# One pass over the weights for both token segments of the residual products

## The chip, the cores and the metric

The kernel runs on one core of a Trainium2 chip. The metric is the time of one execution in device microseconds. On the core, TensorE (PE) multiplies matrices, with a weight load (PEld) beside each multiplication; VectorE (DVE), ScalarE (ACT) and GpSimd (POOL) work elementwise; the queue of SyncE (SP) issues the transfers. Each engine takes its instructions in the order in which the program lists them and waits on semaphores for the others.

## The reference, cut to what matters

Two layers work on 512 latent tokens and 256 context tokens with 1024 features. Each layer has a token mixing and a gated network with a short convolution, and each of the two ends in a residual product. These two products and the norm that follows each are what the change touches:

```
yl = concat([oa_l, ob_l, oc_l, od_l]) @ w_out[l]        # 1024 x 1024
xl = xl + g1 * yl
fl = modulate(rmsnorm(xl, norm_ffn_w[l]), sh2, sc2)
xl = xl + g2 * conv_ffn(fl, ...)                        # ends with @ ffn_w_down[l], 2816 x 1024
if need_ctx:                                            # not in the last layer
    xc = xc + cg1 * (concat([oa_c, ...]) @ w_out[l])    # the same for the context tokens
    ...
return rmsnorm(xl, final_norm_w)
```

The norm divides each token by the root of the mean of its squares over the 1024 features, so none of a token's features can be normed before all eight blocks of 128 features are there.

## The kernel before

Features lie on the partitions, in eight blocks of 128 (m or k = 0 to 7), and tokens along the free dimension. In layer 0 the tokens are two segments, 0 to 512 (latent) and 512 to 768 (context); in layer 1 only the 512 latent tokens are left, in two halves of 256. The residual stream is `x[m]`, 128x768 in float32.

Every product is made in three multiplications per block of 128 features: high part of the weights by high part of the input, high by low, and low by high. A weight unit (128 output features) is loaded by SP as `raw` (three buffers, loaded ahead in the order of `unit_order`), ACT casts it to the high part `wh` (L480), and POOL, or DVE and POOL together in the "fast" form, subtract to get the low part `wl` (L485). `wh` and `wl` have two buffers each; a "spare" unit takes the two buffers of the pool `mrow` instead, which the modulation rows (`mod_dve`, `junk`, L310) of layer 0 use too.

`w_out` (the product after the mixing, name `po`, 24 multiplications per unit and segment) and the last of the chunks of the down product in `ffn` (`pd`, 21 multiplications) run over all eight units for the first segment and then over all eight again for the second. So each unit is loaded, cast and split twice. After each product `residual` (L893, DVE) adds it to `x[m]`.

The norm is a generator, `norm_steps`: the squares `sq` (ACT) and their sums, which PE makes by multiplying with ones (`ms`); then `rstd` (ACT root, DVE reciprocal); then `rb`, the row spread to all partitions (PE); then eight steps of `norm_apply`, each with `yt` (DVE), the high part `yh` (ACT), and the low part `yl`, on DVE for even blocks and on POOL for odd ones (with a second `yt` there). `sq`, `yt` and the rows `up` and `ot` share the pool `u`, which has six buffers. `tick` takes steps of the first segment's norm between the products of the second sweep. With `direct` set, PE sums each square by itself; without it POOL or DVE add them first.

After the second segment's sweep its own norm begins, and `woven` puts the first products of the next stage between its steps: the up product (`pu`) after `w_out`, and the first input products of layer 1 (`pj`) after the down product of layer 0. The order of all this is the order in which the code issues it, apart from small moves by the scheduler.

Of the kernel before, what the change touches and what calls it, by code (L numbers as in the profile page):

```python
# [16 lines left out]
KT = 8  # L17
SEQ = 512
CTX = 256
T = SEQ + CTX  # L20
DEPTH = 2
DFF = 2816
NF = DFF // 128
# [12 lines left out]
SEGS = [(0, SEQ), (SEQ, T)]  # L36
HALVES = [(0, SEQ // 2), (SEQ // 2, SEQ)]
# [5 lines left out]
KEPT = (5, 7)  # L43
HEAD_START = 13
AHEAD_SCORES = 2
SCORE_SHARE = 0.4


# [4 lines left out]
class Trunk:  # L53
# [34 lines left out]
    def build(self):  # L88
# [40 lines left out]
        x = []  # L129
# [5 lines left out]
        steps = [self.rstd_steps(x, *sg, True, "tp", t) for sg, t in zip(SEGS, ("pv", "pj"))]  # L135
# [4 lines left out]
        y = self.new_y()  # L140
# [29 lines left out]
        for l in range(DEPTH):  # L170
            need = l < DEPTH - 1
            NT = T if need else SEQ
            fes.close()
            with ExitStack() as es:
                self.mixing_pools(es)
                todo = []
                if l == 0:
                    todo = list(range(8, 20))
                if l:
                    self.neg_lambda(l)  # L180
                self.mixing(l, y, need, todo)
# [11 lines left out]
            y = None  # L193
            for sg in segs:
                self.w_out(l, s, x, sg)
                y = y or self.new_y()
                steps = self.norm_steps(x, y, sg, self.affn[l], self.mod[l][:, 24:32], sg != segs[0])
                if sg == segs[0]:
                    self.pace = steps
                    self.tick(1)  # L200
            first = [self.up_open(l, 0, gv, True) for gv in range(2)]
            a, b = segs[0]
            part = lambda u, k0, k1: lambda: self.product(u[1][:, a:b], u[0], y, a, b, range(k0, k1))
            self.woven(steps, part(first[0], 0, 4), part(first[0], 4, 8), part(first[1], 0, 8))
            a, b = segs[1]
            self.pin = ALL
            for u in first:
                part(u, 0, 8)()
            self.pin = None
            todo = []  # L210
            if need:
                todo = [lambda j=j: self.mod_dve(0, j, 2) for j in range(40, 48)]
                todo += [lambda j=j: self.mod_dve(1, j, 2 if j < 16 else 1) for j in range(48)]
                self.cbc = self.cp.tile([128, 2, D], F32, name="cbc")
                self.load(self.cbc, d["cbc"], True)
                nc.scalar.activation(out=self.cbc, in_=self.cbc, func=AF.Silu)
            y2 = []

            def after(sg, l=l, need=need, x=x, y2=y2):
                if need:  # L220
                    if not y2:
                        self.scale_vec(l + 1, self.amix[l + 1], O_NM, 8)
                        y2.extend(self.new_y())
                    steps = self.norm_steps(x, y2, sg, self.amix[l + 1], self.mod[l + 1][:, 0:8], sg != segs[0])
                    if sg == segs[0]:
                        self.pace = steps
                        self.tick(1)
                    else:
                        early = self.early_start(l + 1, True)
                        part = lambda n, k0, k1: lambda: self.early_products([early[n]], y2, SEGS[0], range(k0, k1))  # L230
                        self.woven(steps, part(0, 0, 4), part(0, 4, 8), part(1, 0, 8))
                        self.early_products(early[1:], y2, SEGS[1], range(KT))
                        self.split_weights(spare=True)
                    if sg[1] <= SEQ:
                        for k in range(KT):
                            nc.sync.dma_start(out=xd[:, k, sg[0]:sg[1]], in_=x[k][:, sg[0]:sg[1]])
                else:
                    self.pace = self.final(x, sg, sg != segs[0])
                    self.tick(1 if sg == segs[0] else 99)

            self.ffn(l, x, y, segs, first, todo, after)
            y = y2
# [189 lines left out]
    def unit_order(self):  # L432

        for l in range(DEPTH):
            for u in UNITS:
                yield ("win", l, u)
            segs = SEGS if l < DEPTH - 1 else HALVES
            for _ in segs:
                for m in range(KT):
                    yield ("wout", l, m)  # L440
            for k0, k1 in CHUNKS:
                for i in range(k0, k1):
                    if i == 0:
                        yield ("wup", l, 0, 0)
                    yield ("wup", l, i, 1)
                    if i + 1 < NF:
                        yield ("wup", l, i + 1, 0)
                for _ in range(len(segs) if k1 == NF else 1):
                    for m in range(KT):
                        yield ("wdn", l, m, k0, k1)  # L450

    def prefetch(self, depth):
        while len(self.ahead) < depth:
# [284 lines left out]
    def mixing(self, l, y, need, todo):  # L738
# [66 lines left out]
        def score(n):  # L805
            nonlocal at
            for _ in range(n):
                if at < len(scores):
# [4 lines left out]
                    f()  # L813
                    after(w * SCORE_SHARE)

# [81 lines left out]
    def w_out(self, l, s, x, sg):  # L897
        a, b = sg
        for m in range(KT):
            w = self.weights(("wout", l, m), b - a == 256, m % 3 == 2 and l == 0)  # L900
            p = self.bank("tp", "po")
            self.product(p[:, :b - a], w, s, a, b)
            self.residual(p, x, self.mod[l][:, 16:24], m, a, b)
            self.tick(2 if m < 3 else 1)
        self.tick(KT)


    def up_open(self, l, i, gv, fast=False):
# [20 lines left out]
    def ffn(self, l, x, y, segs, first, todo, after):  # L929
        nc = self.nc  # L930
        NT = segs[-1][1]
        cseg = SEGS if NT == T else SEGS[:1]
        gate = self.mod[l][:, 40:48]
        def gate_unit(i):
            ug = self.up(l, i, 0, y, cseg, NT, None if i else first[0])
            nc.scalar.activation(out=ug[:, :NT], in_=ug[:, :NT], func=AF.Silu)
            return ug

        ug = gate_unit(0)
        for k0, k1 in CHUNKS:  # L940
            G = []
            for i in range(k0, k1):
                uv = self.up(l, i, 1, y, cseg, NT, None if i else first[1])
                eng = nc.vector if i == NF - 1 else nc.gpsimd
                cols = [(0, NT)] if eng is nc.vector else [(a, a + 256) for a in range(0, NT, 256)]
                for a, b in cols:
                    eng.tensor_tensor(out=uv[:, a:b], in0=ug[:, a:b], in1=uv[:, a:b], op=ALU.mult)  # L947
                gt = self.g.tile([128, 2, T], F32R, tag="g", name="g")
                nc.scalar.copy(out=gt[:, 0, :NT], in_=uv[:, :NT])
                for a, b in cols:  # L950
                    eng.tensor_tensor(out=gt[:, 1, a:b], in0=uv[:, a:b], in1=f32v(gt[:, 0, a:b]), op=ALU.subtract)  # L951
                G.append((gt[:, 0], gt[:, 1]))
# [5 lines left out]
            sweeps = [[sg] for sg in segs] if k1 == NF else [cseg]  # L958
            for sweep in sweeps:
                for m in range(KT):  # L960
                    w = self.weights(("wdn", l, m, k0, k1), sweep[0][1] - sweep[0][0] == 256,
                                     k1 == NF and m % 3 == 2 and l == 1)
                    for a, b in sweep:
                        p = self.bank("tp", "pd")
                        self.product(p[:, :b - a], w, G, a, b)
                        self.residual(p, x, gate, m, a, b)
                    if todo and m % 2:
                        todo.pop(0)()
                    self.tick(2 if m < 3 else 1)
                self.tick(KT)  # L970
                if k1 == NF:
                    after(sweep[0])


class Group:
# [436 lines left out]
```

## Time and profile before

| | us |
|---|---|
| median of 3 runs | 1759.32 (1756.22 to 1762.36) |
| the profiled execution | 1762.87 |
| its span in the trace | 1761.0 |
| PE busy | 1679.1 (95%) |
| DVE, ACT, POOL busy | 928.5, 787.5, 1017.3 |
| mean granted clock of PE | 0.986 |

The span is what the trace covers; 1.9 us of the execution lie around it. A row of a timeline gives the start, the duration, the engine, the line, what is written from what, and in brackets how long the engine sat idle before it and who released it.

### The profile page before, as it was taken

How to read it: one execution, taken by the hardware profiler on the slowest of the kernel's cores; microseconds unless marked ns; L12 is line 12 of the kernel's file. 1: busy time of each engine (PE TensorE's matmuls, PEld its weight loads, DVE VectorE, ACT ScalarE, POOL GpSimd, SP SyncE). 2: the span in 40 equal slices, each digit the busy share in tenths (PEclk: the TensorE clock that was granted, in tenths of full speed). 3: DMA queues.
4: the chain of work that ended last, by engine and by line, in shares of the span. 5: the costliest groups of instructions: out<-in, count | busy, mean ns of one | idle time of the engine just before them, and what ended most of it. 6: DMA issues, size and time to landing. Idle time of an engine off the chain costs nothing. (4 is left out here: it accounts for less than half of the span.)

```text
span 1761.0 us, 27484 instructions
## 1 busy us (share of the span) xinstructions
PE 1679.1 (95%) x10212; PEld 1448.2 (82%) x10212; DVE 928.5 (53%) x1789; ACT 787.5 (45%) x1355; POOL 1017.3 (58%) x1348
## 2 busy tenths in 40 slices
PE   7899999899999999999999988999999999999997
PEld 4578878798888888888888877888889888888887
DVE  3577767562767644543344566877656522122244
ACT  4377656553533311332133345776654543242343
POOL 1424235766678745775466664424865676676762
PEclk9999999999999999999999999999999999999998
DMA  8675545346533333343334536453436333333334
GB/s 334 177 217 188 156 115 179 93 122 231 168 108 121 124 113 98 120 131 110 119 111 135 181 113 188 138 150 102 147 109 221 106 99 90 102 93 99 96 114 127
DMA packets 78453, 244.21 MB, mean 139 GB/s; under 512 B 9072, under 2 KB 12656, under 8 KB 78192
## 3 DMA queue, kind: packets, MB, share of 16 engines
q1 hardware_dynamic: 78320, 242.46, 43.8%
q8 instruction: 81, 1.33, 0.3%
q14 instruction: 52, 0.43, 0.1%
HBM read 214.64 MB, written 27.79 MB: 138 GB/s over the span
## 5 line engine op out<-in xcount | busy, mean ns | idle before, releaser
L485 POOL TENSOR_TENSOR wl<-raw,wh 128x256 fp32r<-128x256 f32 (+1 forms) x750 | 575.2, 797 | 542.7 <-ACT wh L480 526.5
L480 ACT CAST wh<-raw 128x1024 fp32r<-128x1024 f32 (+1 forms) x228 | 233.5, 1027 | 422.7 <-PE pd L73 194.9
L73 PE MATMUL pu<-yh,wh 128*128 128x512 f32 (+1 forms) x1072 | 377.4, 352 | 1.8 <-DVE up L925 1.8
L73 PE MATMUL pu<-yl,wh 128*128 128x512 f32 (+1 forms) x1072 | 377.2, 352 | 1.8 <-POOL yl L411 1.5
L73 PE MATMUL pu<-yh,wl 128*128 128x512 f32 (+1 forms) x1072 | 376.3, 351 | 0.0
L73 PE MATMUL pd<-g,wh 128*128 128x512 f32 (+1 forms) x1168 | 290.9, 341 | 5.4 <-DVE x L893 2.4
L922 DVE SCALAR_TENSOR_TENSOR up<-pu,par,up 128x511 f32<-128x511 f32 (+1 forms) x132 | 83.0, 657 | 329.0 <-ACT up L920 329.0
L73 PEld LDWEIGHTS pd<-g,wh 128*128 128x128 f32 x1168 | 203.2, 192 | 31.1 <-ACT wh L480 5.6
L73 PEld LDWEIGHTS pu<-yh,wh 128*128 128x128 f32 x1072 | 202.7, 189 | 29.7 <-ACT wh L480 1.5
L73 PEld LDWEIGHTS pu<-yl,wh 128*128 128x128 f32 x1072 | 202.8, 189 | 29.3 <-POOL yl L411 2.1
L73 PEld LDWEIGHTS pu<-yh,wl 128*128 128x128 f32 x1072 | 202.7, 189 | 27.4
L73 PE MATMUL pj<-yh,wh 128*128 128x512 f32 (+1 forms) x608 | 217.4, 361 | 7.2 <-ACT ev L559 4.9
L73 PE MATMUL pj<-yl,wh 128*128 128x512 f32 (+1 forms) x608 | 213.6, 352 | 1.5 <-DVE yl L413 1.4
L73 PE MATMUL pj<-yh,wl 128*128 128x512 f32 (+1 forms) x608 | 212.4, 350 | 0.0
L73 PE MATMUL pd<-g,wl 128*128 128x512 f32 (+1 forms) x584 | 198.4, 341 | 4.6 <-DVE wl L485 4.5
L893 DVE SCALAR_TENSOR_TENSOR x<-pd,mod,x 128x512 f32<-128x512 f32 (+1 forms) x80 | 48.9, 614 | 181.9 <-PE pd L73 181.9
L73 PEld LDWEIGHTS pj<-yh,wh 128*128 128x128 f32 x608 | 117.1, 193 | 26.0 <-ACT ev L559 8.4
L73 PEld LDWEIGHTS pj<-yh,wl 128*128 128x128 f32 x608 | 117.2, 193 | 14.6
L655 POOL TENSOR_TENSOR p<-p,rec 128x512 f32<-128x512 f32 (+2 forms) x80 | 79.5, 997 | 85.6 <-DVE rec L651 62.6
L73 PEld LDWEIGHTS pj<-yl,wh 128*128 128x128 f32 x608 | 117.6, 193 | 13.2 <-DVE yl L413 3.1
L73 PEld LDWEIGHTS pd<-g,wl 128*128 128x128 f32 x584 | 112.3, 192 | 18.0 <-DVE wl L485 5.5
L310 DVE SCALAR_TENSOR_TENSOR junk<-mrow,cbc 128x1024 f32<-128x1024 f32 x80 | 123.2, 1541 | 1.4 <-DMA mrow<-in_wmodt 0.5
(176 smaller groups left out, 2750.5 us busy)
## 6 DMA issues: line engine op xcount, KB each, us to landing
raw<-in_wup SPq DMA_DIRECT2D x88, 512.0 KB, 3.5
mrow<-in_wmodt SPq DMA_DIRECT2D x56, 512.0 KB, 3.8
raw<-in_win SPq DMA_DIRECT2D x44, 512.0 KB, 3.7
raw<-in_wdn SPq DMA_DIRECT2D x48, 448.0 KB, 3.3
mraw<-in_wmod SPq DMA_DIRECT2D x40, 512.0 KB, 7.1
raw<-in_wout SPq DMA_DIRECT2D x32, 512.0 KB, 3.5
qk<-hl SPq DMA_DIRECT2D x16, 768.0 KB, 3.6
stk<-qk SPq DMA_DIRECT2D x32, 384.0 KB, 5.5
```

The lines of the kernel that those rows point to most:

```text
L73: i = self.nc.tensor.matmul(out, **kw)
L310: self.tc.keep_in_program_order(nc.vector.scalar_tensor_tensor(out=junk, in0=raw, scalar=1.0, in1=self.cbc[:, i], op0=ALU.mult, op1=ALU.mu ...
L480: i = nc.scalar.copy(out=wh, in_=raw)
L485: eng.tensor_tensor(out=wl[:, a:b], in0=raw[:, a:b], in1=f32v(wh[:, a:b]), op=ALU.subtract)
L655: self.nc.gpsimd.tensor_tensor(out=p, in0=p, in1=r.broadcast_to(list(p.shape)), op=ALU.mult)
L893: self.nc.vector.scalar_tensor_tensor(out=x[m][:, a:b], in0=p[:, :b - a], scalar=gate[:, m, (0 if b <= SEQ else 1):(1 if b <= SEQ else 2)] ...
L922: nc.vector.scalar_tensor_tensor(out=u[:, a + 1:b], in0=p[:, a:b - 1], scalar=cw[:, 0:1], in1=u[:, a + 1:b], op0=ALU.mult, op1=ALU.add)
```

## The change

`sweep` takes the place of `w_out` and of the last chunk's loop in `ffn`. It goes over the eight units once. For the first six it makes both segments' products while the unit is there (in layer 1 one product of 512 columns in place of two of 256). For the last two (`HELD = 2`, m = 6 and 7) it makes the first segment's product alone and keeps the weights; then the first segment's norm begins (`first_done`), and the two kept units make the second segment's products between its first steps. The last unit is always a spare one, in both layers; no unit of the sweeps has the fast form any more. Both norms now have `direct` set.

```
-            for sg in segs:
-                self.w_out(l, s, x, sg)
-                y = y or self.new_y()
-                steps = self.norm_steps(x, y, sg, ..., sg != segs[0])
-                if sg == segs[0]:
-                    self.pace = steps
-                    self.tick(1)
+            self.sweep(l, lambda m: ("wout", l, m), "po", s, x, self.mod[l][:, 16:24], segs, first_norm)
+            steps = normed(segs[1])
...
+    def sweep(self, l, unit, name, ops, x, gate, segs, first_done, todo=()):
+        whole = segs if segs[1][1] == T else SEGS[:1]
+        def one(m, w, a, b):
+            p = self.bank("tp", name)
+            self.product(p[:, :b - a], w, ops, a, b)
+            self.residual(p, x, gate, m, a, b)
+        kept = []
+        for m in range(KT):
+            w = self.weights(unit(m), spare=m == KT - 1)
+            if m < KT - HELD:
+                for a, b in whole:
+                    one(m, w, a, b)
+            else:
+                one(m, w, *segs[0])
+                kept.append((m, w))
+            if todo and m % 2:
+                todo.pop(0)()
+        first_done()
+        self.tick(1)
+        for m, w in kept:
+            one(m, w, *segs[1])
+            self.tick(1)
+        self.tick(KT + 2)
```

Three places of the order matter for what follows. The first is PE in layer 0, from the end of `w_out` to the first up product, in the kernel before. `po_5796` is the last product of the second sweep, `ms_5838` the second segment's sums of squares, and `yh_5470`, `yl_5471` the first block of the first segment's norm:

```order
L73 MATMUL po_5796<-og_5169,wh_5791 128x256 x2
L73 MATMUL po_5796<-og_5169,wl_5792 128x256
L73 MATMUL ms_5838<-sq_5851,ones_85 32x64 [waits Activation_49]
L73 MATMUL ms_5838<-sq_5851,ones_85 32x64 x3
L73 MATMUL ms_5838<-sq_5857,ones_85 32x64 [waits Activation_49]
L73 MATMUL ms_5838<-sq_5857,ones_85 32x64 x3
L73 MATMUL ms_5838<-sq_5863,ones_85 32x64 [waits Activation_49]
L73 MATMUL ms_5838<-sq_5863,ones_85 32x64 x3
```

and two more such squares follow before `pu_5829`. The same place after the change, where `po_5720` is the kept unit m = 7, `rb_5746` the first segment's row and `ms_5803` the second segment's sums:

```order
L74 MATMUL po_5720<-og_5169,wl_5594 128x256
L74 MATMUL rb_5746<-rstd_5717,ident_83 128x128 [waits DVE_49]
L74 MATMUL rb_5746<-rstd_5717,ident_83 128x128 x3
L74 MATMUL ms_5803<-sq_5804,ones_85 32x64 [waits Activation_49]
...
L74 MATMUL ms_5803<-sq_5840,ones_85 32x64 [waits Activation_49]
L74 MATMUL ms_5803<-sq_5840,ones_85 32x64 x3
L74 MATMUL pu_5794<-yh_5626,wh_5789 128x512
L74 MATMUL pu_5794<-yl_5627,wh_5789 128x512 [waits DVE_49]
```

The row `rb` of the first segment has moved from the middle of the second sweep to a place behind the last product, and all seven of the second segment's sums that stand ahead of the first up product stand behind `rb`.

The second place is ACT at the same point after the change: `yh_5626` to `yh_5640` are the first segment's eight high parts, `sq_5804` to `sq_5846` the second segment's squares.

```order
L411 ACTIVATE yh_5634<-yt_5769,mod0_77 128x512 [waits DVE_49]
L411 ACTIVATE yh_5636<-yt_5773,mod0_77 128x512 [waits DVE_49]
L411 ACTIVATE yh_5638<-yt_5778,mod0_77 128x512 [waits DVE_49]
L347 ACTIVATE sq_5804<-x_5172 128x256 [waits Activation_49]
L347 ACTIVATE sq_5810<-x_5173 128x256 [waits Pool_49]
L347 ACTIVATE sq_5816<-x_5174 128x256 [waits Activation_49]
L347 ACTIVATE sq_5822<-x_5175 128x256 [waits Pool_49]
L347 ACTIVATE sq_5828<-x_5176 128x256 [waits DVE_49]
L347 ACTIVATE sq_5834<-x_5177 128x256 [waits PE_49,Activation_49]
L347 ACTIVATE sq_5840<-x_5178 128x256 [waits PE_49,Activation_49]
L411 ACTIVATE yh_5640<-yt_5782,mod0_77 128x512 [waits DVE_49]
```

The squares stand behind the seventh high part, and the fifth of them waits for a buffer that DVE's last low part, `yl` of block 6, gives back.

The third place is DVE at the end of layer 0's down product after the change, while the first segment's norm for layer 1 is applied; `mrow_10558` is a modulation row, whose buffer held the spare unit m = 7.

```order
L407 SCALAR_TENSOR_TENSOR yt_10692<-x_5172,amix1_80,rb_10687 128x512 [waits PE_49]
L417 SCALAR_TENSOR_TENSOR yl_10566<-yt_10692,mod1_78,yh_10565 128x512 [waits Activation_49]
L407 SCALAR_TENSOR_TENSOR yt_10696<-x_5173,amix1_80,rb_10687 128x512
L407 SCALAR_TENSOR_TENSOR yt_10701<-x_5174,amix1_80,rb_10687 128x512
L314 SCALAR_TENSOR_TENSOR junk_10560,mod1_78<-mrow_10558,cbc_5992 128x1024 [waits DMAHW0_49]
L320 TENSOR_SCALAR mod1_78<-mod1_78,par1_75 128x1 [waits DVE_49]
L417 SCALAR_TENSOR_TENSOR yl_10570<-yt_10701,mod1_78,yh_10569 128x512 [waits Activation_49]
```

A modulation row of 128x1024 and its transfer now stand inside the chain of the norm.

## Rows read from the trace of the kernel before

**Rows 1.** The page, part 1: busy time, share of the span and instructions.
```profile
PE 1679.1 (95%) x10212; PEld 1448.2 (82%) x10212; DVE 928.5 (53%) x1789; ACT 787.5 (45%) x1355; POOL 1017.3 (58%) x1348
```

**Rows 2.** Windows: sweeps and one slow stretch; engines in the order PE, PEld, DVE, ACT, POOL.
```profile
core 0: us, PE busy (x) PEld busy (x) DVE busy (x) ACT busy (x) POOL busy (x), PEclk, DMA share, GB/s
445.40:472.40 27.00, 25.48 (x225) 24.48 (x223) 23.53 (x29) 16.84 (x25) 19.39 (x14) 1.00 0.40 124
1008.00:1040.00 32.00, 25.76 (x209) 23.75 (x207) 26.02 (x33) 17.02 (x27) 20.01 (x16) 0.92 0.40 123
1325.00:1374.40 49.40, 47.70 (x406) 46.27 (x404) 33.65 (x48) 26.54 (x43) 32.25 (x28) 1.00 0.61 194
1702.20:1751.10 48.90, 46.15 (x389) 43.98 (x389) 27.46 (x44) 21.02 (x33) 20.16 (x19) 0.97 0.45 135
1066.40:1072.50 6.10, 6.07 (x29) 6.04 (x29) 2.56 (x4) 0.38 (x1) 2.91 (x5) 0.50 0.65 243
```

**Rows 3.** Timeline of PE in layer 0, from the second sweep into the up product.
```profile
453.24 0.28 PE L73 MATMUL po<-og,wh 128*128 128x256 f32 x1
453.36 0.28 PE L73 MATMUL po<-og,wl 128*128 128x256 f32 x1
...
454.56 1.05 PE L73 MATMUL rb<-rstd,ident 128*128 128x128 f32 x8
...
472.44 0.77 PE L73 MATMUL ms<-sq,ones 128*32 128x64 f32 x40
473.13 0.50 PE L73 MATMUL pu<-yh,wh 128*128 128x512 f32 x1
473.47 0.39 PE L73 MATMUL pu<-yl,wh 128*128 128x512 f32 x1
473.70 0.40 PE L73 MATMUL pu<-yh,wl 128*128 128x512 f32 x1
```

**Rows 4.** Waits of PE, 1008 to 1080 us: for whom, us in total, times, longest.
```profile
PE pj L73 <- ACT ev L559: 3.9, 1, 3.9
PE pd L73 <- DVE wl L485: 3.7, 4, 1.9
```

**Rows 5.** Groups by shape, 453 to 476 us (512-token norm beside a sweep).
```profile
L411 POOL TENSOR_TENSOR yl<-yt,yh 128x512 fp32r<-128x512 f32 x4 | 6.6, 1638 | 0.2
L413 DVE SCALAR_TENSOR_TENSOR yl<-yt,mod,yh 128x512 fp32r<-128x512 f32 x4 | 5.6, 1388 | 0.0
L407 ACT ACTIVATE yh<-yt,mod 128x512 fp32r<-128x512 f32 x8 | 5.5, 717 | 0.7 <-DVE yt L403 0.7
L343 ACT ACTIVATE sq<-x 128x256 f32<-128x256 f32 x8 | 3.0, 410 | 4.3 <-DVE yl L413 3.6 <-POOL yl L411 0.7
```

**Rows 6.** Timeline of DVE: rows of the same norm, and one of a 256-token norm.
```profile
455.65 3.38 DVE L403 SCALAR_TENSOR_TENSOR yt<-x,affn,rb 128x512 f32<-128x512 f32 x5 [0.41 <-PE rb L73]
...
459.68 1.79 DVE L413 SCALAR_TENSOR_TENSOR yl<-yt,mod,yh 128x512 fp32r<-128x512 f32 x1
...
470.07 0.74 DVE L413 SCALAR_TENSOR_TENSOR yl<-yt,mod,yh 128x512 fp32r<-128x512 f32 x1
...
1379.59 2.44 DVE L403 SCALAR_TENSOR_TENSOR yt<-x,affn,rb 128x256 f32<-128x256 f32 x6 [1.53 <-PE rb L73]
```

**Rows 7.** Timeline of POOL: the last low part of that norm.
```profile
473.46 1.30 POOL L411 TENSOR_TENSOR yl<-yt,yh 128x512 fp32r<-128x512 f32 x1
```

**Rows 8.** Groups by shape, 1356 to 1382 us (256-token norms).
```profile
L407 ACT ACTIVATE yh<-yt,mod 128x256 fp32r<-128x256 f32 x13 | 5.8, 497 | 2.6 <-DVE yt L403 2.6
...
L413 DVE SCALAR_TENSOR_TENSOR yl<-yt,mod,yh 128x256 fp32r<-128x256 f32 x5 | 4.2, 832 | 0.0
```

**Rows 9.** The page, part 5: the modulation rows.
```profile
L310 DVE SCALAR_TENSOR_TENSOR junk<-mrow,cbc 128x1024 f32<-128x1024 f32 x80 | 123.2, 1541 | 1.4 <-DMA mrow<-in_wmodt 0.5
```

**Rows 10.** Timeline after the last product of layer 1, all engines.
```profile
1751.06 0.54 PE L73 MATMUL ms<-sq,ones 128*32 128x64 f32 x24
...
1754.76 3.22 DVE L424 SCALAR_TENSOR_TENSOR ot<-x,fin,rb 128x256 f32<-128x256 f32 x8 [1.26 <-PE rb L73]
```

More of the change, by code (lines that the diff above doesn't have):

```diff
@@ L45 @@
 AHEAD_SCORES = 2
+HELD = 2
 SCORE_SHARE = 0.4
@@ L192, in build, with normed, first_norm @@
                     tc.keep_in_program_order(i)
-            y = None
-            for sg in segs:
-                self.w_out(l, s, x, sg)
-                y = y or self.new_y()
-                steps = self.norm_steps(x, y, sg, self.affn[l], self.mod[l][:, 24:32], sg != segs[0])
-                if sg == segs[0]:
-                    self.pace = steps
-                    self.tick(1)
+            y = []
+            def normed(sg):
+                y.extend([] if y else self.new_y())
+                return self.norm_steps(x, y, sg, self.affn[l], self.mod[l][:, 24:32], True)
+            def first_norm():
+                self.pace = normed(segs[0])
+            self.sweep(l, lambda m: ("wout", l, m), "po", s, x, self.mod[l][:, 16:24], segs, first_norm)
+            steps = normed(segs[1])
             first = [self.up_open(l, 0, gv, True) for gv in range(2)]
@@ L223, in after @@
                         y2.extend(self.new_y())
-                    steps = self.norm_steps(x, y2, sg, self.amix[l + 1], self.mod[l + 1][:, 0:8], sg != segs[0])
+                    steps = self.norm_steps(x, y2, sg, self.amix[l + 1], self.mod[l + 1][:, 0:8], True)
                     if sg == segs[0]:
                         self.pace = steps
-                        self.tick(1)
                     else:
@@ L237, in after @@
                 else:
-                    self.pace = self.final(x, sg, sg != segs[0])
-                    self.tick(1 if sg == segs[0] else 99)
+                    self.pace = self.final(x, sg, True)
+                    if sg != segs[0]:
+                        self.tick(99)
             self.ffn(l, x, y, segs, first, todo, after)
@@ L436, in unit_order @@
                 yield ("win", l, u)
[L437 to L440, printed above, removed]
+            for m in range(KT):
+                yield ("wout", l, m)
             for k0, k1 in CHUNKS:
@@ L447, in unit_order @@
                         yield ("wup", l, i + 1, 0)
-                for _ in range(len(segs) if k1 == NF else 1):
-                    for m in range(KT):
-                        yield ("wdn", l, m, k0, k1)
+                for m in range(KT):
+                    yield ("wdn", l, m, k0, k1)
     def prefetch(self, depth):
@@ L895, in residual @@
                                             in1=x[m][:, a:b], op0=ALU.mult, op1=ALU.add)
-    def w_out(self, l, s, x, sg):
-        a, b = sg
-        for m in range(KT):
[L900 to L905, printed above, removed]
+    def sweep(self, l, unit, name, ops, x, gate, segs, first_done, todo=()):
[5 more added lines that the diff above has]
+        kept = []
+        for m in range(KT):
+            w = self.weights(unit(m), spare=m == KT - 1)
[13 more added lines that the diff above has]
+        self.tick(KT + 2)
     def up_open(self, l, i, gv, fast=False):
@@ L957, in ffn @@
                     ug = gate_unit(i + 1)
[L958 to L972, printed above, removed]
+            if k1 == NF:
+                self.sweep(l, lambda m: ("wdn", l, m, k0, k1), "pd", G, x, gate, segs, lambda: after(segs[0]), todo)
+                after(segs[1])
+                continue
+            for m in range(KT):
+                w = self.weights(("wdn", l, m, k0, k1))
+                for a, b in cseg:
+                    p = self.bank("tp", "pd")
+                    self.product(p[:, :b - a], w, G, a, b)
+                    self.residual(p, x, gate, m, a, b)
+                if todo and m % 2:
+                    todo.pop(0)()
 class Group:
```

## The prediction

> **What bounds the kernel now.** I read the busy shares first: PE is busy for 1679.1 of 1761.0 us, every other engine for under 60% [rows 1]. So a cast, a split or a load that goes away gives nothing by itself. What counts is the time in which PE stands or runs slowly, and whether the change takes such time away or makes it.
>
> I then cut windows around the sweeps that the change rebuilds [rows 2]. The second sweep of the layer-0 output product takes 27.0 us with PE busy for 25.48; that of the layer-0 down product 32.0 us with 25.76 and a granted clock of 0.92; the two sweeps of the layer-1 output product together 49.4 us with 47.70; the two of the layer-1 down product 48.9 us with 46.15 and a clock of 0.97. The waits say what is late: in the layer-0 down sweep DVE's half of the split, 3.7 us in four waits [rows 4]. DVE makes the split and the norm at once there, so the weights come late.
>
> The third view is PE's timeline at the end of such a sweep: sums from 472.44, and at 473.13 the first up product with no idle bracket [rows 3]. The norm of the first segment, from 455.65 [rows 6] to 473.46 + 1.30 = 474.76 us on POOL [rows 7], some 19 us, lies almost wholly beside the second sweep. It costs PE only the losses inside that sweep. That cover is what the change takes away.
>
> **What it saves.** A multiplication of 256 columns starts 0.12 us after the one before it, one of 512 columns 0.23 (473.47 to 473.70) [rows 3]. For each sweep I set two bounds: PE's idle time in the window, and everything in the window beyond its products, which also holds sums and `rb` that stay.
> - Layer-0 output: 8 x 24 x 0.12 = 23.0. Idle 1.5, all beyond 4.0. I take 2.2.
> - Layer-0 down: 8 x 21 x 0.12 = 20.2. Idle 6.2, all beyond 11.8. I take 9.5, as idle time leaves out what the lower clock costs.
> - Layer-1 output: 16 x 24 x 0.12 = 46.1. Idle 1.7, beyond 3.3. I take 2.2. Six of eight units become 512 wide: 6 x 24 x (0.24 - 0.23) = 1.4. Together 3.6.
> - Layer-1 down: 16 x 21 x 0.12 = 40.3. Idle 2.8, beyond 8.6. I take 5.7 and 6 x 21 x 0.01 = 1.3, together 7.0.
>
> The sum is 22.3 us, with 15 and 26 as ends. The 32 unit loads, casts and splits that go are inside it, as what made PE late. In the new pass the whole split is POOL's, but a layer-0 unit now feeds 24 x (0.23 + 0.12) = 8.4 us of PE, twice the work of the 256-column sweep per weight, so I cost the loss of the fast form at nothing. If weights still came late, at most the 2 us or so of a single wait [rows 4] would come back per pass.
>
> **What it costs: the norm without its cover.** The only cover left is the two kept units: 2 x 24 x 0.12 = 5.8 us in an output product and 2 x 21 x 0.12 = 5.0 in a down product. The squares of m = 7, `rstd` and its reciprocal fit beside that. Then `rb` follows, and behind it the order lists 28 sums of the second segment's squares ahead of the first up product. On ACT these squares come after the seventh `yh`, and the fifth of them needs the buffer that DVE's `yl` of block 6 gives back. PE is in order. So it stands from `rb` until seven of eight blocks have been applied. In the kernel before, the same sums stood there too, but nothing of the first segment's norm was left to wait for by then.
>
> The chain, for 512 columns, from the start of `rb`:
> - to the first `yt`: 455.65 - 454.56 = 1.1 us [rows 3, 6]
> - seven `yt` on DVE at 3.38 / 5 = 0.68, with some at 0.74: 4.9 [rows 6]
> - four `yl` on DVE at 1.39 while POOL works beside it: 5.6 [rows 5]. Alone such a row takes 0.74, the longest beside POOL 1.79 [rows 6], so 3.0 to 7.2.
> - four times DVE waits for ACT's `yh`, 0.72 each: 2.9 [rows 5]
> - three squares behind the last `yl`, chained, at most 0.41 each: 1.1 [rows 5]
>
> That is 15.6. About 1.0 of it is PE's own `rb` and sums, which the kernel before also has, so the new idle time is 14.5 us after the layer-0 output product; with the ends for `yl` 12 to 16.
>
> After the layer-0 down product the same norm runs for layer 1's input product. The kept units end 0.8 us sooner while the norm does not. The order puts a modulation row between two steps on DVE, 1.54 us [rows 9], with its transfer behind the spare unit; and a spare unit's split stands on POOL between the first `yt` and `yl`, which gives back some 0.7 us more. 14.5 + 0.8 + 1.5 + 0.7 = 17.5 us, between 14.5 (the row is ready and hidden) and 20.
>
> After the layer-1 output product the segments are halves of 256: 1.1 + 7 x 2.44 / 6 [rows 6] + 4 x 0.83 + 4 x 0.50 [rows 8] + 1.0 = 10.3, less PE's own 0.7, gives 9.6 us (8 to 11).
>
> The three gaps sum to 41.6 us.
>
> **The clock behind a gap.** In the kernel before, PE waits 3.9 us for `ev` [rows 4], and the following 6.1 us run at a granted clock of 0.50 [rows 2], that is at 1.2 GHz: half of it, 3.05 us, is lost. Three new gaps, each longer than that one, may each bring such a stretch. I take 7.5 us for the three, 0 and 9.2 as ends.
>
> **The end of layer 1.** From the last product to the end of the span it takes 1761.0 - 1751.06 = 9.9 us [rows 10]. After the change the first half's norm has not been applied by then: its eight `ot` rows of 3.2 us [rows 10] and the second half's squares, which wait for buffers that the output transfers free, come behind the kept products. I take +3 us, the `ot` rows; between 0 and 5.
>
> **The sum.** 41.6 + 7.5 + 3 - 22.3 = +29.8 us. The profiled execution before is 1762.87 us (1.9 of it outside the span), so the same execution after is 1792.7. The profiled execution is 3.6 above the median of the runs, which gives 1789 us.
>
> **A rule of the Trainium skill against the middle of the chain.** In rows 5 a `yl` on DVE beside POOL takes 1.39 us where one alone takes 0.74, and a `yl` on POOL 1.64. The Trainium skill, page "SBUF — State Buffer", section "SBUF: two separate sides", says that a DVE instruction with two SBUF inputs and a GpSimd instruction that reads SBUF share a port pair under an exclusive lock, and that whoever comes second is blocked for the whole instruction of the other. By that rule each `yl` on the chain, which has POOL's `yt` and `yl` beside it all the time, may stand for a whole POOL instruction. It gets a rival below; the longest row, 1.79, speaks for less than that.
>
> **Rivals.**
> 1. The norm stays hidden. The sums do not hold PE, as at 473.13 before, and the kept products cover what must be there first. Then only savings and the tail remain: -22.3 + 3, about 1740 us. It decides if the three gaps together are under 12 us, 4 us each. For it speaks that PE met no wait at 473.13; against it that the norm had 19 us of sweep beside it then, and has 5 to 6 now. Chance 0.06.
> 2. PE waits only for blocks as they come. If the second segment's squares found buffers early, the first up product would run beside the application, and each gap would shrink by that product: 24 x 0.23 = 5.5 twice, 24 x 0.12 = 2.9 once. With 3 us for the clock: 41.6 - 13.9 + 3 + 3 - 22.3 = +11.4, about 1771 us. The pool of six buffers and ACT's order speak against it. Chance 0.10.
> 3. A short chain at full clock. DVE's `yl` run alone at 0.74, 2.6 us less in each of the two wide gaps, and no slow stretch follows: 1789 - 5.2 - 7.5 = 1776 us. The slow stretch after only 3.9 us of waiting speaks against it. Chance 0.10.
> 4. The lock in full. A `yl` waits 1.64 for POOL's row and then takes 0.74, that is 2.38 in place of 1.39: 4 x 1.0 x 2 = +8, about 1797 us. Chance 0.10.
>
> My forecast has 0.64. A change of 0.3% (5 us) is about what a measurement of this kernel can tell from none. Rival 1 lies on the faster side; the lower half of rival 2's spread reaches the band of no change; the forecast and rivals 3 and 4 are all slower. That gives 0.07 faster, 0.05 the same, 0.88 slower. The range takes in rivals 2 to 4, with the ends of `yl` and the clock: 1771 to 1803 us.
>
> **What would show it.** PE's timeline should show an idle bracket of 12 to 16 us at the sums `ms` ahead of the first up product of layer 0, released by ACT's `sq`; one of 14 to 20 after the layer-0 down product; one of 8 to 11 in layer 1; each followed by a granted clock near 0.5 for some microseconds. The window of the layer-0 down product should hold no wait for `wl`. The time from the last product to the end should be about 13 us. The prediction is wrong if PE goes into the first up product with under 5 us of idle time, if the new single pass waits for its weights (POOL makes them alone), or if the slow clock costs far more than 3 us a gap.

## The result and the profile after

The changed kernel takes 1801.13 us (median of 5 runs, 1796.68 to 1804.36) against 1759.32 before: 1.0238 times as long, with a 95% interval of 1.0222 to 1.0255. The forecast was 1789 with a range of 1771 to 1803. The direction and the mechanism held; of 42 us, 12 were not forecast. The profiled execution after is 1801.13 us, span 1799.3, which is 38.3 above the span before. The forecast for this pair of profiled executions was 29.8, so 8.5 us of the miss can be looked for in the traces; the other 3.6 are what the profiled execution before lies above the median of its runs.

The page, part 1, after; it answers to [rows 1]:

```profile
PE 1689.9 (94%) x10166; PEld 1437.3 (80%) x10166; DVE 863.1 (48%) x1721; ACT 760.3 (42%) x1324; POOL 974.4 (54%) x1344
```

The other engines have less to do, by 65, 27 and 43 us on DVE, ACT and POOL: the reloaded units are gone, and so are the adds of the first segment's squares. PE is busy for 10.8 us more, which the page alone can't explain. PE's timeline in layer 0, from the end of the output product to the first up product, answers to [rows 3]:

```profile
474.92 0.28 PE L74 MATMUL po<-og,wl 128*128 128x256 f32 x1
475.60 1.16 PE L74 MATMUL rb<-rstd,ident 128*128 128x128 f32 x8 [0.40 <-DVE rstd L361]
487.66 1.05 PE L74 MATMUL ms<-sq,ones 128*32 128x64 f32 x24 [10.91 <-ACT sq L347]
489.94 1.36 PE L74 MATMUL ms<-sq,ones 128*32 128x64 f32 x32 [1.22 <-ACT sq L347]
491.23 0.80 PE L74 MATMUL pu<-yh,wh 128*128 128x512 f32 x1
```

Where there was no bracket, PE now stands for 10.91 and 1.22 us at the second segment's sums, released by ACT's squares. The same place after the down product of layer 0, and then after the output product of layer 1:

```profile
1053.49 1.16 PE L74 MATMUL rb<-rstd,ident 128*128 128x128 f32 x8 [0.76 <-DVE rstd L361]
1066.35 0.44 PE L74 MATMUL ms<-sq,ones 128*32 128x64 f32 x8 [11.70 <-ACT sq L347]
1068.40 0.75 PE L74 MATMUL ms<-sq,ones 128*32 128x64 f32 x16 [1.61 <-ACT sq L347]
1070.74 1.36 PE L74 MATMUL ms<-sq,ones 128*32 128x64 f32 x32 [1.59 <-ACT sq L347]
1072.03 0.80 PE L74 MATMUL pj<-yh,wh 128*128 128x512 f32 x1
...
1400.30 1.10 PE L74 MATMUL rb<-rstd,ident 128*128 128x64 f32 x8
1408.48 1.06 PE L74 MATMUL ms<-sq,ones 128*32 128x64 f32 x24 [7.08 <-ACT sq L347]
...
1411.48 0.58 PE L74 MATMUL pu<-yh,wh 128*128 128x256 f32 x1
```

To see where all 38.3 us went, I cut both spans at the same starts in PE's timeline (last product or attention row `pv` of a stage, first product of the next). The last column is a version from the experiments, with the first segment's squares added before PE sums them; its numbers and those of the column "after" are differences to the kernel before.

| stretch ending at | before, us | after | after, sums pre-added |
|---|---|---|---|
| last `pv` of layer 0 | 403.09 | +1.5 | +1.6 |
| last `po` | 69.14 | +1.2 | -2.8 |
| first `pu` | 0.91 | +15.4 | +14.3 |
| last `pu` | 495.58 | +1.0 | +1.6 |
| last `pd` of layer 0 | 70.96 | -6.3 | -10.9 |
| first `pj` of layer 1 | 1.36 | +18.2 | +18.1 |
| last `pv` of layer 1 | 283.88 | -1.5 | +2.1 |
| last `po` | 49.33 | -3.7 | -6.6 |
| first `pu` | 0.90 | +10.6 | +9.6 |
| last `pu` | 326.77 | +2.1 | +1.5 |
| last `pd` | 48.93 | -4.8 | -8.7 |
| end of the span | 10.15 | +4.7 | +5.4 |

The two stretches up to `pv` hold no code that the change touches. In the profiles of the runs below, which all have the same code there, the first of them lies between 2.0 us less and 4.3 more than before, so 1.5 says nothing. The three gaps cost 15.4 + 18.2 + 10.6 = 44.2 us, near the 41.6 of the forecast. The surprise stands in the second row: the pass over the output weights, which was to save 2.2 us, got longer. No product of the four passes waits for a low part of the weights, so the splits, now all on POOL, are not the reason.

### The profile page after: what moved, and what is told of

It reads as the page before. It is cut to its first block, busy times and chain, and to the rows that moved or that the text cites. A ratio compares the mean times of both kernels' runs of the same rounds, so it can differ in the third digit from the quotient of the medians.

```text
span 1799.3 us, 27044 instructions
## 1 busy us (share of the span) xinstructions
PE 1689.9 (94%) x10166; PEld 1437.3 (80%) x10166; DVE 863.1 (48%) x1721; ACT 760.3 (42%) x1324; POOL 974.4 (54%) x1344
## 5 line engine op out<-in xcount | busy, mean ns | idle before, releaser
L486 POOL TENSOR_TENSOR wl<-raw,wh 128x256 fp32r<-128x256 f32 (+1 forms) x766 | 558.0, 760 | 594.0 <-ACT wh L481 587.2
L481 ACT CAST wh<-raw 128x1024 fp32r<-128x1024 f32 (+1 forms) x196 | 202.1, 1033 | 397.5 <-PE pd L74 183.6
L74 PE MATMUL pd<-g,wh 128*128 128x512 f32 (+1 forms) x1084 | 284.2, 352 | 1.9 <-DVE x L894 0.8
L74 PEld LDWEIGHTS pd<-g,wh 128*128 128x128 f32 x1084 | 190.3, 189 | 31.4 <-ACT wh L481 1.5
L74 PE MATMUL pd<-g,wl 128*128 128x512 f32 (+1 forms) x542 | 189.8, 352 | 0.1
L966 POOL TENSOR_TENSOR up<-up 128x256 f32<-128x256 f32 x105 | 117.0, 1139 | 1.1 <-DVE up L944 0.6
```

The lines of the kernel that those rows point to most:

```text
L74: i = self.nc.tensor.matmul(out, **kw)
L481: i = nc.scalar.copy(out=wh, in_=raw)
L486: eng.tensor_tensor(out=wl[:, a:b], in0=raw[:, a:b], in1=f32v(wh[:, a:b]), op=ALU.subtract)
```

## The experiments

Ratios are to the kernel before, with their 95% intervals; it was run again beside each group of experiments, at medians of 1758.3 to 1759.7 us. Differences in us are between medians, a microsecond or two of which can come from the group.

**Six sums left out.** In `rstd_steps`, with the squares still made:

```
-                if k < KT - 1:
+                if k < (1 if a == 0 and self.slow else KT - 1):
                     sums(sq, k == 0, False)
```

> The changed kernel with six of the eight sums of squares left out in every norm of a first segment (their squares are still made, the first and the last are still summed; the norm's values are therefore other ones). My theory for the 8 us by which I forecast too little: both norms sum directly, and each square that PE now sums in the pass stands on PE's path: 0.36 us of four small multiplications in layer 0, 0.25 in layer 1, which I costed at nothing. Then 2 x 6 x 0.36 + 2 x 6 x 0.25 = 7.3 us go, the run lies about 1794 where the changed kernel lies at 1801, and the idle times before the first up product stay at about 12, 15 and 8 us. Rival: the sums are hidden or the extra time lies in the clock behind the gaps: then the run stays within 2 us of 1801.

1787.2 us, 1.0161 (1.0141 to 1.0181): 14 us less than the changed kernel, about twice the 7.3 that I worked out. The idle times in front of the first products stayed (the stretch to the first `pu` in layer 0 is +15.4 as before). In its profile the four passes get 2.9, 3.4, 2.5 and 3.4 us shorter, 12.2 for 24 sums, that is 0.51 a sum, and PE's busy time falls to 1677.2 us, below the 1679.1 of the kernel before. So the sums stand on PE's path, they explain why PE was busier, and each costs more than its own row.

**Squares added first.**

```
-                return self.norm_steps(x, y, sg, ..., True)
+                return self.norm_steps(x, y, sg, ..., sg != segs[0])
...
-            w = self.weights(unit(m), spare=m == KT - 1)
+            w = self.weights(unit(m), spare=m == KT - 1 and (name, l) != ("pd", 0))
...
-            self.tick(1)
+            self.tick(2 if i < 3 else 1)
```

and the same as the first pair for the other two norms.

> The changed kernel with one thing undone: the first segment's squares are added by GpSimd and VectorE before PE sums them once, as in the kernel before. Theory (direct sums stand on PE's path): 2 x 7 x 0.36 + 2 x 7 x 0.25 = 8.5 us less on PE, less what the last adds put into the chain ahead of the row rb (up to 1 us a place, 3 to 4 in all): about 1795 us, 1793 to 1798. Rival (the sums cost nothing, what was missed is the clock): about 1801 or a little more.

1784.7 us, 1.0147 (1.0128 to 1.0166): 16 us less. More than one thing was undone, though: the last unit of layer 0's down product also lost its spare buffer (the edit of "No spare unit" below, which alone gave 2 us), and two steps of the norm follow each kept unit. So the 16 us are not the price of the sums alone. Its timeline shows the price of one sum, where the other edits have no part. First a unit of the changed kernel's pass in layer 0, from its start to the next one's:

```profile
420.93 0.73 PE L74 MATMUL po<-og,wh 128*128 128x512 f32 x2
...
429.48 0.42 PE L74 MATMUL ms<-sq,ones 128*32 128x128 f32 x6
429.83 0.73 PE L74 MATMUL po<-og,wh 128*128 128x512 f32 x2
```

and then the same unit with the squares added first:

```profile
420.65 0.63 PE L75 MATMUL po<-og,wh 128*128 128x512 f32 x2
...
428.99 0.63 PE L75 MATMUL po<-og,wh 128*128 128x512 f32 x2
```

8.90 us a unit with a sum, 8.34 without: 0.56, where the sum itself takes 0.35 from its start to the next product. The four passes get 3.9 + 4.5 + 2.8 + 3.9 = 15.1 us shorter than in the changed kernel (the table's numbers before rounding).

**The sums alone, in the kernel before.** `sg != segs[0]` becomes `True` at its three norms.

> The kernel before with one thing of the change alone: the first segment's norms sum each square on PE, in place of adding the squares on GpSimd and VectorE first. Taking these sums out of the changed kernel gave 14 and 16 us, about twice what the rows of the sums themselves (0.36 and 0.25 us) make. Theory: a sum between two wide products costs PE 0.55 us in layer 0 (a unit of the pass takes 8.90 us where its products make 8.35) and about 0.4 in layer 1, so 14 x 0.55 + 14 x 0.4 = 13.3 us on PE's path here too: 1769 to 1774 us. Rival: VectorE and GpSimd, rid of the adds, give back what PE loses, and the 14 us belong to the one-pass form alone: under 1765 us.

1772.5 us, 1.0076 (1.0054 to 1.0098): 13.4 us, as forecast. The cost does not hang on the one-pass form. In its profile the stretches add up to less: 10.9 us in the span, 3.5 of it ahead of any norm. The stretches of the four products are 2.0, 4.7 and 2.3 us longer and, for the last one, 0.7 shorter, some 8 in all. So the size is less sure here than in the changed kernel.

**The product ahead of the second segment's sums.**

```
-            self.woven(steps, part(first[0], 0, 4), part(first[0], 4, 8), part(first[1], 0, 8))
+            self.pin = ALL
+            part(first[0], 0, 8)()
+            self.pin = None
+            self.woven(steps, part(first[1], 0, 1), part(first[1], 1, 4), part(first[1], 4, 8))
```

and likewise for layer 1's input products.

> The changed kernel with the second segment's sums issued behind the first product of the next stage in place of ahead of it, at all three places. Theory: the sums ahead of the product hold PE until seven blocks are applied; then the idle time in front of the first product falls from about 12, 15 and 8 us to under 4 (until the first high part is there), PE takes the blocks as they come, and the end of the first product, now set by the last low part on GpSimd, comes 3 us sooner at each place; part of it goes to the second segment's norm, which begins later. 1792 to 1799 us. If the sums did not hold PE, the idle time in front of the product stays and the run is at 1801. If the product is covered wholly by the application (the rival of my prediction at -14), about 1787.

1794.5 us, 1.02 (1.0181 to 1.0218): 6.6 us less, inside the forecast. PE's waits in it from 472 to 515 us:

```profile
PE pu L74 <- POOL yl L421: 4.2, 5, 2.1
PE pu L74 <- ACT yh L417: 2.3, 2, 1.6
PE pu L74 <- DVE up L950: 1.4, 1, 1.4
PE pu L74 <- DVE yl L423: 0.7, 2, 0.4
```

The order did hold PE: no wait for a square is left at the three places. But the blocks of the norm come at their own pace, and PE now waits for them one by one, most for POOL's `yl`. The stretch to the first `pu` falls from +15.4 to +2.5, and the one behind it rises by 10.8. Most of the gap is the uncovered application, and where the sums stand is worth the 6.6 us.

**Filled gaps.** 44, 56 and 28 multiplications of 512 columns behind `rb`, in the pass's end:

```
+            for i in range(n):
+                self.mm(p, lhsT=self.identr, rhs=ops[0][0][:, :512], start=i == 0, stop=i == n - 1)
```

> The changed kernel with multiplications of 512 columns in the three gaps, between the row rb and the second segment's sums (44, 56 and 28 of them, some 80% of each gap; their result is read by nobody). Theory: the gap is as long as before, as ACT's squares end it, but PE's clock does not fall, so the sums and the first product run at full clock: 1.5, 1.4 and 2.0 us less at the three places, about 5 us in all: 1796 us. Rival (the clock behind a gap costs 7.5, as I predicted): 1793 or less; rival (the slow stretch is no part of the path): 1801.

1799.3 us, 1.0239 (1.021 to 1.0269): no difference that can be told from the changed kernel's 1.0238. The windows say why. In the changed kernel, behind the three gaps (columns as in [rows 2]):

```profile
491.20:498.30 7.10, 7.10 (x34) 5.43 (x31) 0.55 (x1) 0.84 (x3) 2.32 (x2) 0.76 0.00 0
1072.00:1081.20 9.20, 9.20 (x48) 7.30 (x45) 1.52 (x4) 1.44 (x4) 2.32 (x2) 0.85 0.01 2
1411.50:1418.00 6.50, 6.50 (x46) 6.11 (x43) 0.56 (x2) 0.31 (x1) 0.43 (x1) 0.64 0.00 0
```

and with the gaps filled, a gap and then the same three places:

```profile
474.50:489.90 15.40, 13.15 (x109) 10.04 (x109) 9.12 (x13) 7.45 (x15) 7.97 (x6) 1.00 0.26 100
489.90:497.00 7.10, 7.10 (x34) 5.41 (x31) 0.55 (x1) 0.91 (x3) 2.31 (x2) 0.76 0.01 2
...
1070.80:1080.00 9.20, 9.20 (x48) 7.36 (x45) 1.46 (x4) 1.40 (x4) 2.32 (x2) 0.84 0.00 0
...
1411.10:1417.50 6.40, 6.40 (x66) 6.16 (x59) 2.42 (x6) 1.69 (x6) 1.20 (x3) 1.00 0.00 0
```

The clock was full inside the gap, and fell in layer 0 all the same behind it; only in layer 1 it stayed full, and the up stretch there lost its 2.1 us (+0.1 in place of +2.1). In layer 0 the filling ended some microseconds ahead of the product, with waits and small sums between. Whether a filling up to the last sum would have kept the clock there was not tried.

**One unit kept.** `HELD = 1`.

> The changed kernel with one unit kept in place of two. In the changed kernel PE waits 0.4 to 0.8 us for rstd ahead of the row rb, so the two kept products cover just the reduction (squares, sums, rstd), and nothing of the application behind rb. Theory: with one kept product (2.9 or 2.5 us) the reduction sticks out by about 2 us at each place, so +1.5 to 2 at four places, 1807 to 1809 us, and the idle time behind rb stays at 12.1, 14.9 and 7.6 us. Rival: the kept products cover the norm as a whole, and each one taken away shows in full (2.9 + 2.5 + 2.9 + 2.5): 1812 us.

1804.2 us, 1.0259 (1.0243 to 1.0276): 3 us more, which the intervals do not tell apart, below both expectations and far from the rival's 11. The waits for `rstd` ahead of `rb` grew from 0.4, 0.8 and none to 1.5, 3.5 and 1.0 us. Those behind it stayed at 12.1 and 7.6 at the first and third place; at the second, against the expectation, they fell from 14.9 to 12.2, where DVE now makes the modulation row before it begins to apply the norm. PE's waits in it from 1035 to 1085 us:

```profile
PE ms L74 <- ACT sq L347: 12.2, 2, 11.0
PE rb L74 <- DVE rstd L361: 3.5, 1, 3.5
```

By the profile the three stretches to the first product and the end are 1.4, 1.2, 1.2 and 1.9 us longer. So a kept product covers the reduction, and nothing of the application.

**No spare unit in layer 0's down product.** `spare=m == KT - 1 and (name, l) != ("pd", 0)`.

> The changed kernel, but the last unit of layer 0's down product takes an ordinary weight buffer and no spare one, so that the modulation row and its transfer no longer stand inside the first segment's norm, nor the split of the third input unit. Theory: the chain behind rb there shrinks from 18.5 by the row (1.54) and the split in POOL's way (0.7) to some 16.3 us, unless the first input units now come late: 1797 to 1800 us against 1801. Rival: the row was hidden beside other work of the chain: no change.

1799.0 us, 1.0226 (1.0208 to 1.0244), not told apart from the changed kernel by the interval. Its place shows the effect: from `rb` at 1054.01 to `pj` at 1069.64, 15.6 us in place of 18.5, with the same brackets as after the output product, while the pass itself takes 0.5 us more:

```profile
1054.01 1.16 PE L74 MATMUL rb<-rstd,ident 128*128 128x128 f32 x8 [0.76 <-DVE rstd L361]
1066.08 1.05 PE L74 MATMUL ms<-sq,ones 128*32 128x64 f32 x24 [10.91 <-ACT sq L347]
1068.35 1.36 PE L74 MATMUL ms<-sq,ones 128*32 128x64 f32 x32 [1.22 <-ACT sq L347]
1069.64 0.80 PE L74 MATMUL pj<-yh,wh 128*128 128x512 f32 x1
```

**Two units in one pass, six behind.** In the pass `if m < 2` both segments, m = 6 and 7 kept, then m = 2 to 5 loaded again, their split shared between DVE and POOL. Layer 0's down product has no spare last unit, and two steps of the norm follow the first three units behind.

> A form between the two kernels: only the first two units of each sweep make both segments' products in one pass, the last two are kept, the middle four are loaded again for the second segment, and the kept ones go first in it; sums as in the kernel before. Theory (the cost is the norm's lost cover): six units of the second segment, 17.3 us in an output product and 15.1 in a down product, cover most of the first segment's norm, so that the gaps shrink to 0 to 6 us in layer 0 and nothing in layer 1, while half of the reloads and about half of the losses of the two-sweep form (11 of 22 us) go: 1747 to 1757 us. Rival (the losses in the second sweep come from the norm sharing DVE and POOL with any split, not from the reloads): 1757 to 1765.

1779.3 us, 1.011 (1.009 to 1.0129). It missed by more than 20 us. The gaps did shrink (to 6.6 us before the first `pu` of layer 0), but the three stretches to the first products are still 5.7, 6.0 and 3.4 us longer than before. Losses inside the second sweep went in layer 0's down product (6.6 us shorter) and not in layer 1's output product, where PE waits 3.7 us once for a residual:

```profile
1363.01 4.65 DVE L487 TENSOR_TENSOR wl<-raw,wh 128x640 fp32r<-128x640 f32 x1 [2.69 <-ACT wh L482]
...
1366.26 0.72 POOL L357 TENSOR_TENSOR sq<-sq 128x256 f32<-128x256 f32 x1
...
1367.59 0.47 DVE L895 SCALAR_TENSOR_TENSOR x<-po,mod,x 128x256 f32<-128x256 f32 x1
...
1368.12 0.79 PE L75 MATMUL po<-og,wh 128*128 128x256 f32 x2 [3.68 <-DVE x L895]
```

The residual stands on DVE behind its half of a split, which takes 4.65 us, where its median in the kernel before is 0.83. POOL has row after row beside it, and the split ends 0.7 us after the last of them (1366.26 + 0.72 = 1366.98). A second such split, of 4.00 us, stands in layer 1's down product. Fewer reloads alone do not pay for less cover. How the rest divides among the waits stays open: the profiled execution (1786.9 us) lies 7.6 above the median of the runs, so its trace sizes little.

**The pass where no product waits.** From the kernel before, one pass in layer 1's down product alone, squares added on POOL and DVE during the pass (`last_sweep` is not shown):

```
+            if k1 == NF and l == DEPTH - 1:
+                self.last_sweep(l, lambda m: ("wdn", l, m, k0, k1), G, x, gate, after)
+                continue
```

> The kernel before with the one pass in the layer-1 down product alone, its squares added by GpSimd and VectorE during the pass for both halves, so that after the last product only the last two squares of the second half are left to sum. Theory: the pass saves what it saved in the changed kernel without direct sums (40.3 us from the first up product's end to the last product in place of 48.9, -8.6), as no next product waits for this norm, and the end costs the eight ot rows of the first half, 2 to 3 us: 1752 to 1755 us. Rival: the end costs 5 us or more as in the changed kernel, which leaves 1756 to 1760.

1754.2 us, 0.9979 (0.9967 to 0.999). The pass saves 8.65 us (40.27 in place of 48.93) and the end costs 3.7, where PE's last row `rb` waits:

```profile
1738.08 1.10 PE L73 MATMUL rb<-rstd,ident 128*128 128x64 f32 x8
1739.12 0.32 PE L73 MATMUL ms<-sq,ones 128*32 128x64 f32 x8
1743.05 1.94 PE L73 MATMUL rb<-rstd,ident 128*128 128x64 f32 x8 [3.62 <-DVE rstd L942]
```

**Modulation rows earlier.** `range(2)` becomes `range(2 if i < 10 else 3)` in the up loop, on top of that.

> The version above, and the twelve modulation rows that VectorE computes during layer 0's down product are issued during its up products in place of there (three per unit from the tenth unit on). Theory: the second sweep of layer 0's down product loses its 10 us because VectorE has norm, splits and four modulation rows of 1.54 us at once; without the rows the waits for wl (3.7 us) and some of the slow clock go: 4 to 7 us less than the version above, 1746 to 1751 us. Rival: the norm beside GpSimd's split is enough to be late: less than 2 us.

1756.1 us, 0.9982 (0.997 to 0.9994): no gain. The waits for `wl` in the down product fell from 3.2 to 2.4 us, and a wait of 2.6 us for the squares came at its end.

**The last reciprocal earlier.** On top of the one-pass version in layer 1's down product alone, the reciprocal pinned behind four of the eight `ot` rows.

> The version with one pass in the layer-1 down product alone (1754 us), with the second half's reciprocal on VectorE issued after four of the first half's eight ot rows in place of behind all of them. There PE waits 3.6 us for rstd ahead of the last rb. Theory: four rows of 0.40, 1.6 us, go from the end: 1752 to 1753 us, the end from the last product 12.2 us in place of 13.9. Rival: the output transfers set the end: no change.

1753.0 us, 0.9972 (0.9959 to 0.9984). This is the lowest median of all, ahead of both kernels, though its interval overlaps that of the version before it (0.9967 to 0.999); the end is 13.4 us in place of 13.8. Only 0.4 of the 1.6 us came: `rb` now waits for the `ot` rows, which still read the one bank that it is to write.

```profile
1744.75 1.44 PE L73 MATMUL rb<-rstd,ident 128*128 128x64 f32 x8 [3.53 <-DVE ot L951]
```

**Kept units first in the other second sweeps.** Order 6, 7, 0 to 5, with 6 and 7 from the first sweep. Which units take the spare buffers changes with it.

> The version before it, and in the other three second sweeps the first sweep's last two units are kept and used first, so that six units in place of eight are loaded and split again. Theory: the second sweep's losses come from splits beside the norm, so a quarter of 2.5, 9.5 and 3.4 us goes, 3 to 4 us less than the version before it, about 1749 us. Rival: the losses come from the norm's order on DVE and ACT (the two-in-one form lost 4 us to a residual that stood behind norm rows): no gain, or up to 5 us more.

1758.8 us, 0.9999 (0.9989 to 1.0009): the gain of the version before it is lost again, 5.9 us. The trace places 1.3 us of it at each of the two first `pu` and 2.4 at the first `pj` of layer 1, less 2.8 us that come back in two of the sweeps; the rest is not placed. So the theory fell. The rival's size is about met, but its reason is not shown, and the residual that it points to stood behind a split, as seen above.

## Why the prediction was right, and where its sizes were off

- **The mechanism.** PE stands behind `rb` at the second segment's sums, at three places. The forecast gave 15.6, 17.8 and 10.3 us from the start of `rb` to the first product (the second with the modulation row and the split; the 0.8 of earlier readiness lies ahead of `rb` and is seen there as a wait of 0.76). Measured are 15.63, 18.54 and 11.18. Of this PE is idle for 12.1, 14.9 and 7.6 us, less than the 14.5, 17.5 and 9.6 forecast, the last below its range of 8 to 11. The rest is PE's own `rb` and sums, put at 1.0 and taking 3.5 at the first place, where the granted clock from 486 to 492 us was 0.50. Rival 1 fell with the first bracket. Rival 2 had its mechanism tested: with the order changed the kernel gained 6.6 us and no more.
- **Inside the chain two errors cancelled.** DVE's rows there, and POOL's first:

```profile
476.79 0.75 DVE L407 SCALAR_TENSOR_TENSOR yt<-x,affn,rb 128x512 f32<-128x512 f32 x1 [0.95 <-PE rb L74]
478.33 0.75 DVE L417 SCALAR_TENSOR_TENSOR yl<-yt,mod,yh 128x512 fp32r<-128x512 f32 x1 [0.79 <-ACT yh L411]
479.00 1.40 DVE L407 SCALAR_TENSOR_TENSOR yt<-x,affn,rb 128x512 f32<-128x512 f32 x2
480.57 1.04 POOL L413 TENSOR_TENSOR yt<-yt,mod 128x512 f32<-128x512 f32 x1 [5.96 <-ACT yh L411]
481.18 0.97 DVE L417 SCALAR_TENSOR_TENSOR yl<-yt,mod,yh 128x512 fp32r<-128x512 f32 x1 [0.79 <-ACT yh L411]
```

  The four `yl` take 3.7 us, not 5.6 as taken from [rows 5], where DVE had splits between. And the last four squares waited not for DVE's `yl` of block 6, which ends at 488.31, but for POOL, whose `yl` of block 5 ends at 489.44. ACT's order under the change shows this wait too: the fourth square, `sq_5822`, waits for POOL.

```profile
487.84 1.60 POOL L415 TENSOR_TENSOR yl<-yt,yh 128x512 fp32r<-128x512 f32 x1
...
489.47 1.34 ACT L347 ACTIVATE sq<-x 128x256 f32<-128x256 f32 x4 [1.25 <-POOL yl L415]
```

  From DVE's last `yl` to the first product 2.9 us pass, where 1.1 was taken. So 1.9 too much and 1.8 too little meet, and that 15.63 comes so near to 15.6 is luck.
- **The modulation row and the split** were put at 1.5 + 0.7 us; without both the place is 2.9 us shorter. The trace gives most of it to the split. From the first `yt` to the end of its last `yl`, DVE takes 12.1 us at the second place, row included, and 11.5 at the first. On POOL four splits stand between the norm's rows there, and the squares wait for POOL twice:

```profile
1063.33 1.86 POOL L486 TENSOR_TENSOR wl<-raw,wh 128x256 fp32r<-128x256 f32 x2
...
1070.27 1.34 ACT L347 ACTIVATE sq<-x 128x256 f32<-128x256 f32 x4 [1.61 <-POOL yl L415]
```

- **The step that failed: the sum of savings.** It treated the sums as work that stays. With `direct` set on both norms PE sums seven more squares at each of four places, 28 in all, and that was costed at nothing. Without 24 of them the changed kernel is 14 us faster; in the kernel before all 28 cost 13.4. At 0.51 a sum the 28 make 14 us, more than the whole miss.
- **The savings themselves** were larger than forecast where they can be seen without the sums: 2.8, 6.6 and 8.7 us in the layer-0 output and both layer-1 products, against 2.2, 3.6 and 7.0. Layer 0's down product, forecast at 9.5, saves 10.9 in that version, with its other edits, and 9.7 with six sums left out. That gave some 6 us back. (The unit that feeds PE for 8.4 us has nearly three times the 2.9 of the 256-column sweep, not twice; nothing hangs on it, as no product waited for a split.)
- **The clock** behind the gaps cost less than the 7.5 taken: 7.1 x 0.24 + 9.2 x 0.15 + 6.5 x 0.36 = 5.4 us in the windows above. The stretches there, up to the last `pu`, the last `pv` of layer 1 and the last `pu` again, are 1.0 longer, 1.5 shorter and 2.1 longer, 1.6 in all, though such a stretch up to `pv` scatters.
- **The end** cost 4.7 us, inside 0 to 5, where 3 was taken. The last squares wait for a buffer that an output transfer reads, as the forecast had it:

```profile
1788.78 0.72 ACT L347 ACTIVATE sq<-x 128x256 f32<-128x256 f32 x2 [0.88 <-DMA out<-ot]
...
1791.11 1.94 PE L74 MATMUL rb<-rstd,ident 128*128 128x64 f32 x8 [1.11 <-DVE rstd L361]
```

- **The sum, by the profiled pair.** 38.3 - 29.8 = 8.5 us were not forecast. As an estimate from the terms above: +14.3 for the sums, -5.7 for the savings (the table's 13.7 and the 14.3, less 22.3), +2.6 for the gaps, +1.7 for the end, -5.9 for the stretches behind the gaps, and the 1.5 ahead of any change, which is scatter. That the measured time fell inside the range thus owes something to errors of both signs.
- **Rival 3** had half of its premise right: the `yl` on DVE ran near their time alone. But the way to the first product was no shorter, for POOL set the end of it, and the slow clock came.
- **Rival 4** (the lock in full, 2.38 us a `yl`) fell by its price: three of the four `yl` on DVE took 0.97 us, with POOL's rows of 1.04 and 1.60 around them. The page "SBUF — State Buffer" of the Trainium skill, section "SBUF: two separate sides", has one of the two engines blocked for the whole instruction of the other. This chain does not speak against that: when the second `yl` starts at 481.18, POOL's `yt` beside it has 0.43 us left (480.57 + 1.04 - 481.18), not 1.64. The split of 4.65 us in the version with two units in one pass, which ended only behind POOL's last row, agrees with the rule. So the rule has a price where POOL's rows follow one another without a break, and it had a small one here.

## What to carry to other kernels

A second sweep that reloads its weights may be the cheapest cover for a norm: before it goes, write down what lies beside it, and read from each engine's order what the next product must then wait for. Flags that ride along with a change (here the direct sums) are part of its price; count their instructions on the bound engine, and not by their own rows alone. Make the one pass where nothing waits for the norm that follows: that gave 0.2%, and 0.3% with the reciprocal moved.

## What the runs showed of the hardware

A group of four small sums (eight records in the trace) between two wide products cost PE 0.56 us in the pass, while the time from its first row to the next product is 0.35. DVE's half of a split, 0.83 us at the median, took 4.65 where POOL ran row after row beside it, and ended 0.7 us after POOL's last. And filling a gap with multiplications kept the granted clock at 1.00 inside it, but the next product in layer 0 still ran at 0.76 over its first 7 us, after some microseconds of small sums and waits.
